# An S5 mixer in rounds on one Trainium2 core: y loaded by GpSimd, weights and rounds regrouped, heads transposed one tile later

## The chip, the core and the metric

The kernel runs on one core of one Trainium2 chip. Its engines are TensorE (PE in the profile, with its weight loads as PEld), VectorE (DVE), ScalarE (ACT), GpSimd (POOL) and SyncE (SP); ACT, POOL and SP also issue DMAs. The metric is the device time of one launch in microseconds (us), the median of several runs.

## The reference

A trunk of two layers on x (1024 tokens by 1024 features, float32). Each sub-layer is a RMS norm with shift, scale and gate from a conditioning vector c. Cut to what matters here:

```python
def _s5_mixer(h, w_in, ..., D, w_glu, b_glu, w_out):
    u, z = jnp.split(h @ w_in, 2, axis=-1)
    ...
    _, _, s_r, s_i = lax.associative_scan(_cplx_combine, (a_r, a_i, bu_r, bu_i), axis=1)
    y = einsum(s_r, C_re) - einsum(s_i, C_im) + D * u      # 64 groups of 16 channels, 64 states each
    y = jax.nn.gelu(y)
    y = y * jax.nn.sigmoid(y @ w_glu + b_glu)
    y = y * jax.nn.silu(z)
    return y @ w_out

x = x + gate * s5(x)
k, v, F = shared_kv(x, c)      # k per head RMS normed
x = x + gate * fox(x, k, v, F) # q = h @ w_in per head RMS normed; attention with forget gates F
```

## The kernel before

Every large product is made of float32 operands split in two: a high part by a copy on ACT (aH, w_hi, wvh) and a low part by a subtraction on DVE (aL, w_lo, wvl), and three matmuls for each block of 128 (high by high, low by high, high by low). The program has these stages in time: a prelude (statistics, the modulation of c, tables of powers); the S5 stage with the projections u and z; the gate projection (pj_g); the output projection (pj_o); values, then keys, then queries (tkps, token tiles); the attention with z of the second layer filled in; the last projection.

**The S5 stage.** The 1024 channels make eight groups, and round e works on group e (`for e in range(KT)`). In a round:
- DVE runs `scan` (L687, over the chunks of 8 tokens, NCH = 128 of them), whose result has its two halves of 64 partitions swapped by two DMAs of SP (`swap_halves`, `DMA v<-v` in the profile). It runs `products` for later groups: wm, and moa, in halves hb = 0 and 1. `rotate_back` (L218, the tensor r) needs the swap. `tables` makes sines of the turning angle: xhi + ylo, then a rounding by adding and taking off a large number (L598) and a subtraction, so that the angle lies in half a turn either way; ACT then takes Abs, Sin, Sin.
- PE runs `turn_in` (transposes of wm, tensor pin, L634), `taps` (pk, L646, reads moa), `states_in` (vps), and `states_out` (py, L706, reads r and moa).
- ACT applies GELU to py, and POOL stores the result to DRAM in eight DMAs (`y_d<-r`, L714).

Between these PE fills in the projections u of groups 1 to 7 and then z of groups 0 to 7, which don't depend on the round. A strip of 128 columns of u or z (L266) has three chunks, of 258, 512 and 256 columns, 24 matmuls each; `unit(n)` puts n chunks at a place of the round. A round has three or four of them. A chunk of u is scaled into `et` by DVE (L374); one of z is copied into `ez` by ACT (L406), two `ez` sharing three buffers with `et`, and each half strip of z is stored by a DMA of SP (`z_d<-ez`). A strip's weights come as `weight_strip` (L87 load, L95 w_hi, L103 w_lo), where the scheduler places them.

**What sets the order.** A tile framework schedules the program: instructions go to their engine's queue in an order that it chooses, and buffers and data give the waits. Two chains written by hand bind it: `ve` puts the DVE steps of the rounds in a row, `te` the PE steps (`order[0]`, `order[1]`). `tc.issue_after(x)` makes what is issued within it stand behind x in the order; it is no wait on a result. Each engine takes its queue in order.

**After the rounds**, the GELU'd y is loaded back (`yl`, eight DMAs of 128x1024 floats, L797), behind the last load of u in the order, split into aH and aL, and multiplied by the gate weights (pj_g, L114).

**Keys and queries** (L941 tkps, L965 hsq, L970 hnt, L977 trps, L981 kh). A token tile is 24 matmuls of 256 columns into PSUM; ACT squares it (hsq), DVE reduces, POOL makes the inverse root, DVE writes the normed tile hnt, which frees the PSUM. When four token tiles are done, `qk_half` transposes them on PE (trps), and ACT and DVE write high and low parts (kh, kl), which are stored. While queries begin, ACT also makes aH of the modulated inputs (L186) and wvh, the high part of the next wide weights (L924), DVE the low part wvl (L925).

Of the kernel before, what the change touches and what calls it, by code (L numbers as in the profile page):

```python
# [20 lines left out]
P = 128  # L21
# [25 lines left out]
def trunk(tc, a, out):  # L47
# [3 lines left out]
    with top:  # L51
# [155 lines left out]
        with l0:  # L207
# [23 lines left out]
            tpi = halves("tpi", 2 * PI_LO, -2 * PI_LO)  # L231
# [135 lines left out]

            def width(c):
                return 512 if c == 0 else 256
# [7 lines left out]
            def u_strip(e, w=None, done=(), ets=(), tags=(None,) * 3):  # L377
                w = w or weight_strip(a["a_w_in"][e], [P, KT, P])
                ut = s5.tile([P, TC, NCH], F32, name="ut", tag="ut")
                bi = s5.tile([P, 1], F32, name="bi", tag="bi", bufs=3)  # L380
                for c in (2, 0, 1):
                    et, m = None, None
                    if c < 2 and ets:
                        et = ets[c]
                    else:
                        ps, m = (done[c], None) if c < 2 and done else chunk(w, c, f"u{e}", tags[c])
# [77 lines left out]

            turn = ta
            S.activation(turn[:, 1:], th[:, 1:], AF.Copy, scale=1.0 / (2 * math.pi))
            turn = [turn[:, i + 1].unsqueeze(2) for i in range(7)]
            ylo = s5.tile([P, NG, 16], F32, name="ylo", tag="ylo")
            xhi = s5.tile([P, NG, 8], F32, name="xhi", tag="xhi")
            S.activation(ylo[:, :, 0:1], turn[0], AF.Copy, scale=-1.0)  # L470
# [115 lines left out]
            def swap_halves(o, x, q=S):  # L586
                for hh in range(2):
                    q.dma_start(out=o[64 * hh:64 * hh + 64], in_=x[64 - 64 * hh:128 - 64 * hh])


            def tables(e, st):
# [6 lines left out]
                V.tensor_scalar(out=cT, in0=sT, scalar1=MAGIC, scalar2=-MAGIC, op0=ALU.add, op1=ALU.add)  # L598
# [77 lines left out]
            def scan(e, st):  # L676
# [12 lines left out]
                swap_halves(r3, r2, Q)  # L689
# [8 lines left out]
            def states_out(e, st, sin):  # L698
# [14 lines left out]
                for i in range(TC):  # L713
                    G.dma_start(out=y_d[e, :, i, :].rearrange("(c g) k -> c g k", c=GC), in_=yb[GC * i:GC * i + GC])  # L714
                st.clear()
                return end

            loaded, sts, order = [], [{} for _ in range(KT + 2)], [None, None]
# [10 lines left out]
            def te(f, *xs):  # L729
                with behind(1):  # L730
                    order[1] = f(*xs)
# [4 lines left out]

            load_u(0, sts[0])
            unit(2)
# [12 lines left out]
            unit()  # L751
            for e in range(KT):
# [3 lines left out]
                unit()  # L756
                if more:
# [3 lines left out]
                    unit(2)  # L761
                    ve(products, e + 1, 1, b_)
                    te(turn_in, 1, b_)
                    te(taps, e + 1, 1, b_)
# [5 lines left out]
                if e % 2 == 0 or not more:  # L770
                    unit(1 if more else 3)
# [21 lines left out]
            for k in range(KT):  # L793
                pool, tag = ((s5, "bb"), (s5, "bbs"), (s5, "x1m"), (s5, "x2m"), (sbm, "min_"), (s5, "ut"), (sb, "uu"), (sb, "uu"))[k]
                yls.append(pool.tile([P, TC, NCH], F32, name=f"yl{k}", tag=tag, bufs=2 if tag == "uu" else 1))
                with tc.issue_after(loaded[-1]):
                    last_y = Q.dma_start(out=yls[k], in_=y_rows(k)).ins  # L797
# [5 lines left out]
            wg = [weight_strip(a["a_w_glu"][e], [P, KT, P], V) for e in range(2)]  # L803
# [102 lines left out]
        with l1a:  # L906
# [9 lines left out]

            wide_dma, last_kl, last_nt, last_sq, last_pow = [], [], [], [], []

            def wide(src, f_src=None):
# [4 lines left out]
                S.activation(wh[:, :, 0:256], raw, AF.Copy)  # L924
                V.tensor_tensor(out=wl[:, :, 0:256], in0=raw, in1=wh[:, :, 0:256].bitcast(F32), op=ALU.subtract)  # L925
# [7 lines left out]
            def token_tile(w, t, nv=256):  # L933
# [4 lines left out]
                for k in range(KT):  # L938
                    hh, ll = act[0][k][i][:, c0:c0 + P], act[1][k][i][:, c0:c0 + P]
                    for at, wt in ((hh, wh), (hh, wl), (ll, wh)):  # L940
                        T.matmul(ps[:, 0:nv], at, wt[:, k, 0:nv], start=(n == 0), stop=(n == 3 * KT - 1))  # L941
                        n += 1
# [17 lines left out]
            def qk_tile(w, t):  # L960
# [8 lines left out]
                nt = hp.tile([P, 4, HD], F32, name="hnt", tag="hnt", bufs=5)  # L969
# [64 lines left out]
            for j, job in enumerate(("v0", "v2", "k0", "k2", "q0", "q2")):  # L1034
# [19 lines left out]
                for i in range(2):  # L1054
# [7 lines left out]
                    for d in range(2):  # L1062
                        nts = []
                        for t in range(4 * i, 4 * i + 4):
# [24 lines left out]
                        if kind != "v":  # L1089
# [6 lines left out]
                            qk_half(nts, gain, 2 * (n0 + d), i, k_d if kind == "k" else q_d)  # L1096
# [281 lines left out]
```

## Time and profile before

| | |
|---|---|
| median of 3 runs | 1177.03 us (1174.55 to 1177.37) |
| the profiled execution | 1175.35 us, span 1173.5 us |
| mean granted TensorE clock | 0.995 |
| busy: PE, DVE, ACT, POOL | 97%, 71%, 52%, 30% |
| S5 rounds, first scan to the gate projection | 107.88 to 293.31 us |
| bytes read and written in DRAM | 138.21 and 46.27 MB |

The span runs from the first to the last instruction; the profiled execution's time has 1.85 us more around it. Engines are listed by busy time, and a group of instructions by its line, engine, operation and tile. Behind a group or an instruction stands the idle time of its engine just before it, with what ended it. In a table of windows each engine's busy us stands with its instructions; the last three columns are the granted clock (1.00 is full), the share of the DMA engines and the GB/s that they moved.

### The profile page before, as it was taken

What the parts mean: (1) busy time and instruction counts of PE and PEld (TensorE: products, weight loads), DVE (VectorE), ACT (ScalarE), POOL (GpSimd) and SP (SyncE); (2) the same over time, 40 slices, a digit from 0 to 9 for tenths busy, and PEclk for the clock granted to TensorE, in tenths of its full rate; (3) what the DMA queues carried; (4) which work ended last, traced back from release to release, by engine and by line L of the source; (5) the groups of instructions that cost most, each with busy time, mean ns of one, the idle gap of its engine ahead of it and who ended that gap; (6) DMA issues with size and microseconds to landing.
All of it is one profiled execution on the core that took longest, in us unless ns stands there. A gap on an engine that the chain in (4) does not pass through costs nothing.

```text
span 1173.5 us, 20611 instructions
## 1 busy us (share of the span) xinstructions
PE 1142.8 (97%) x7506; PEld 1016.8 (87%) x7506; DVE 838.1 (71%) x1723; ACT 605.7 (52%) x1141; POOL 347.1 (30%) x572
## 2 busy tenths in 40 slices
PE   9999999998999999999999999999999999999998
PEld 7688888888888787999999999988988898887886
DVE  6768999885788875935867755348888888898431
ACT  6665777665533432522332533247777777787210
POOL 2300112112000153211343345434455544544100
PEclk9999999999999999999999999999999999999999
DMA  9664577686875783148853339236565554641151
GB/s 354 214 192 133 143 175 171 152 212 182 303 252 198 264 289 121 72 170 281 301 182 132 114 122 273 105 126 132 114 135 129 125 125 111 150 103 63 53 173 72
DMA packets 94661, 197.11 MB, mean 168 GB/s; under 512 B 17728, under 2 KB 42496, under 8 KB 93024
## 3 DMA queue, kind: packets, MB, share of 16 engines
q1 hardware_dynamic: 86768, 174.17, 50.1%
q0 software_dynamic: 6048, 16.85, 4.7%
q10 hardware_dynamic: 1744, 4.77, 1.8%
q8 instruction: 59, 0.97, 0.3%
q14 instruction: 42, 0.34, 0.1%
HBM read 138.21 MB, written 46.27 MB: 157 GB/s over the span
## 4 chain that ended last, share of the span: by engine, by line
PE 70%; DVE 12%; ACT 8%; DMA 5%; issue 3%; POOL 0%; SPq 0%; ACTq 0%; DVEq 0%
PE tkps L941 23%; PE pj_g L114 7%; PE zb L114 6%; PE pj_o L114 6%; PE pj_f L114 4%; PE tp L1185 4%; PE u L266 3%; PE ov L1191 3%; PE f L114 3%; PE ov L1192 2%; PE sp L1152 2%; PE sp L1153 2%; DMA v<-v 2%; ACT pr L1160 2%; DVE r L218 2%
## 5 line engine op out<-in xcount | busy, mean ns | idle before, releaser
L941 PE MATMUL tkps<-wvh,aH 128*128 128x256 f32 (+1 forms) x768 | 220.1, 287 | 3.3 <-DVE hnt L970 3.3
L941 PE MATMUL tkps<-wvl,aH 128*128 128x256 f32 (+1 forms) x768 | 216.6, 282 | 0.0
L941 PE MATMUL tkps<-wvh,aL 128*128 128x256 f32 (+1 forms) x768 | 216.0, 283 | 0.0
L941 PEld LDWEIGHTS tkps<-wvh,aH 128*128 128x128 f32 x768 | 145.2, 189 | 4.1 <-DVE hnt L970 3.7
L941 PEld LDWEIGHTS tkps<-wvl,aH 128*128 128x128 f32 x768 | 145.3, 189 | 0.3 <-issue 0.2
L941 PEld LDWEIGHTS tkps<-wvh,aL 128*128 128x128 f32 x768 | 144.9, 189 | 0.5 <-DVE hmod L183 0.2
L1162 POOL TENSOR_SCALAR pr<-pr,sm 128x128 f32<-128x128 f32 (+7 forms) x128 | 95.2, 750 | 92.7 <-DVE sm L1161 92.6
L1187 ACT ACTIVATE pth<-tp 128x512 fp32r<-128x512 f32 (+1 forms) x192 | 86.8, 489 | 50.5 <-PE ov L1191 29.5
L1160 ACT ACTIVATE pr<-pr,mx 128x128 f32<-128x128 f32 (+7 forms) x128 | 98.9, 774 | 24.9 <-DVE mx L1157 23.9
L1188 DVE TENSOR_TENSOR ptl<-tp,pth 128x512 fp32r<-128x512 f32 (+1 forms) x192 | 101.0, 551 | 9.7 <-ACT pth L1187 8.8
L714 POOL DMA_DIRECT2D y_d<-r x64 | 33.4, 550 | 199.2 <-ACT r L709 198.1
L1157 DVE CUSTOM_DVE_ANT_0 pr<-sp,msk 128x512 f32<-128x512 f32 (+3 forms) x128 | 72.6, 569 | 21.4 <-PE tp L1185 15.5
L1185 PE MATMUL tp<-ident,pr 128*128 128x128 f32 x576 | 82.1, 273 | 2.6 <-DVE ptl L1188 2.6
L1191 PE MATMUL ov<-pth,vhl 128*128 128x256 f32 x320 | 84.1, 296 | 0.3
L965 ACT ACTIVATE hsq<-tkps 128x256 f32<-128x256 f32 x64 | 24.4, 384 | 115.1 <-PE tkps L941 112.5
L95 ACT ACTIVATE w_hi<-w_raw 128x1024 fp32r<-128x1024 f32 x47 | 49.6, 1055 | 64.8 <-PE pj_f L114 19.8
L1192 PE MATMUL ov<-ptl,vhl 128*128 128x256 f32 x320 | 79.7, 283 | 0.2
L1185 PEld LDWEIGHTS tp<-ident,pr 128*128 128x128 f32 x576 | 68.6, 140 | 12.3 <-DVE ptl L1188 2.0
L968 POOL TENSOR_TENSOR hms<-hms,nhalf 128x4 f32<-128x4 f32 x64 | 70.8, 1106 | 5.3
L1152 PE MATMUL sp<-kk,qs 128*128 128x256 f32 (+2 forms) x192 | 69.9, 367 | 0.6 <-DVE mx L1157 0.5
L1153 PE MATMUL sp<-kk,q 66*128 66x256 f32 (+2 forms) x192 | 65.6, 345 | 0.0
L266 PE MATMUL z<-aH,w_hi 128*128 128x258 f32 (+2 forms) x192 | 62.7, 327 | 1.4 <-ACT ez L406 1.4
(356 smaller groups left out, 3154.2 us busy)
## 6 DMA issues: line engine op xcount, KB each, us to landing
modw<-modw SPq DMA_DIRECT2D x48, 512.0 KB
wvr<-kvq_w SPq DMA_DIRECT2D x12, 1024.0 KB
w_raw<-a_w_in SPq DMA_DIRECT2D x16, 512.0 KB
v_d<-vt POOLq DMA_DIRECT2D x32, 256.0 KB, 4.1
kk<-k_d SPq DMA_DIRECT2D x16, 512.0 KB
vhl<-v_d SPq DMA_DIRECT2D x16, 512.0 KB
qs<-q_d SPq DMA_DIRECT2D x32, 256.0 KB
w_raw<-a_w_out SPq DMA_DIRECT2D x10, 512.0 KB
```

Source lines behind the costliest of these rows:

```text
L114: m = T.matmul(ps, w[wt][:, k, :], act[at][k][half], start=(k == k0 and n == 0), stop=(k == k1 and n == 2)).ins
L266: m = T.matmul(ps[:, 0:c1 - c0], w[wt][:, k, :], act[at][k][i][:, c0:c1], start=(k == 0 and n == 0), stop=(k == KT - 1 and n == 2)).ins
L941: T.matmul(ps[:, 0:nv], at, wt[:, k, 0:nv], start=(n == 0), stop=(n == 3 * KT - 1))
L1152: T.matmul(sp[:, 0:wm_], qsl, kk[:, 0, lo:lo + wm_], start=True, stop=False)
L1153: sp_end.append(T.matmul(sp[:, 0:wm_], q1_[:, P * i:P * i + P], kk[0:HD + 2, 1, lo:lo + wm_], start=False, stop=True).ins)
L1160: S.activation(pr[:, 0:nk], pr[:, 0:nk], AF.Exp, scale=-1.0, bias=mx, accum_out=sm)
L1162: G.tensor_scalar(out=pr[:, 0:nk], in0=pr[:, 0:nk], scalar1=sm, scalar2=0.0, op0=ALU.mult, op1=ALU.add)
L1185: T.transpose(out=tp[:, b, :], in_=prs[qi][:, P * (b0 + b):P * (b0 + b) + P], identity=ident)
L1187: S.activation(pth[:, 0:m, dst], tp[:, 0:m, :], AF.Copy)
L1188: V.tensor_tensor(out=ptl[:, 0:m, dst], in0=tp[:, 0:m, :], in1=pth[:, 0:m, dst].bitcast(F32), op=ALU.subtract)
L1191: T.matmul(ov, vhl[:, b, :], pth[:, b - b0, :], start=(b == 0), stop=False)
L1192: end = T.matmul(ov, vhl[:, b, :], ptl[:, b - b0, :], start=False, stop=(b == nb - 1)).ins
```

## The change

It has four parts.
- **Rounds.** A chunk of u or z is now made in two halves of four blocks (`chunk2`, 12 matmuls each), and `unit` counts halves: seven in a round, with one of them between the second `turn_in` and `taps`. A strip's weights are tied into the DVE chain (`load_weights`): the next strip's are loaded, and their parts made, where a strip begins.
- **Wrapped turns.** The angles are kept in 0 to -1 turns, wrapped after each addition by one operation ((s <= -1) + s, L483 after), in place of the rounding by a large number and its subtraction. ACT's three operations get other scales and biases. The small tables xhi and ylo of the prelude are wrapped after each of their five additions.
- **y's loads.** Seven of the eight yl are issued by GpSimd, in the order behind the stores of round 6 (the seventh), the eighth by SP; of the last round's eight stores four go to SP. The gate's first weights stand behind the last round's swap in the order.
- **Keys and queries.** `qk_half` of four token tiles is issued behind the matmuls of the next job's first token tile, and not at once (`turned`); wvh and wvl are made in two halves each; hnt has six buffers for five.

```diff
+            def chunk2(w, c, nm):
+                ps = pj.tile([P, HL], F32, name=f"{nm}_{c}", tag="pj")
+                for r in range(2):
+                    yield ps, in_part(ps, w, c, range(KT // 2 * r, KT // 2 * r + KT // 2))
...
             def z_strip(e):
-                w = weight_strip(a["a_w_in"][8 + e], [P, KT, P], l_eng=V)
+                w = next_weights()
...
-                    ps, m = chunk(w, c, f"z{e}")
+                    two = chunk2(w, c, f"z{e}")
+                    yield next(two)[1]
+                    ps, m = next(two)
...
+            def wrap(o, s):
+                return V.scalar_tensor_tensor(out=o, in0=s, scalar=-1.0, in1=s, op0=ALU.is_le, op1=ALU.add)
...
                 tt(t[:, :, m:2 * m], t[:, :, 0:m], turn[i].broadcast_to([P, NG, m]), ALU.add)
+                wrap(t[:, :, m:2 * m], t[:, :, m:2 * m])
...
-                V.tensor_scalar(out=cT, in0=sT, scalar1=MAGIC, scalar2=-MAGIC, op0=ALU.add, op1=ALU.add)
-                end = tt(sT, sT, cT, ALU.subtract)
-                S.activation(cT, sT, AF.Abs)
-                S.activation(cT, cT, AF.Sin, scale=-2 * PI_LO, bias=hpi)
-                st["sin"] = S.activation(sT, sT, AF.Sin, scale=tpi).ins
+                end = wrap(sT, sT).ins
...
+                S.activation(cT, sT, AF.Abs, bias=half)
+                S.activation(cT, cT, AF.Sin, scale=2 * PI_LO, bias=nhpi)
+                st["sin"] = S.activation(sT, sT, AF.Sin, scale=ntpi, bias=npi).ins
...
-                    G.dma_start(out=y_d[e, :, i, :].rearrange("(c g) k -> c g k", c=GC), in_=yb[GC * i:GC * i + GC])
+                    q = Q if e == KT - 1 and i % 2 else G
+                    stored[e] = q.dma_start(out=y_d[e, :, i, :].rearrange("(c g) k -> c g k", c=GC), in_=yb[GC * i:GC * i + GC]).ins
+                    if q is Q:
+                        stored[KT] = stored[e]
...
+            def load_weights(e):
+                with behind(0):
+                    in_w.append((e, weight_strip(a["a_w_in"][e], [P, KT, P])))
+                order[0] = parts[1].ins
...
+            def next_weights():
+                if not in_w:
+                    load_weights(U_FIRST)
+                e, w = in_w.pop(0)
+                if e + 1 < 2 * KT:
+                    load_weights(e + 1)
+                return w
...
                 ve(scan, e, a_)
-                unit()
+                unit(2)
                 if more:
                     load_u(e + 1, b_)
                     te(turn_in, 0, b_)
                     te(taps, e + 1, 0, b_)
-                    unit(2)
+                    unit(3)
                     ve(products, e + 1, 1, b_)
                     te(turn_in, 1, b_)
+                    unit()
                     te(taps, e + 1, 1, b_)
...
-                if e % 2 == 0 or not more:
-                    unit(1 if more else 3)
+                unit(1 if more else 6)
...
-                with tc.issue_after(loaded[-1]):
-                    last_y = Q.dma_start(out=yls[k], in_=y_rows(k)).ins
+                with tc.issue_after(stored[KT if k == KT - 1 else KT - 2]):
+                    last_y = (Q if k == KT - 1 else G).dma_start(out=yls[k], in_=y_rows(k)).ins
...
-            wg = [weight_strip(a["a_w_glu"][e], [P, KT, P], V) for e in range(2)]
+            with tc.issue_after(swapped[0]):
+                wg = [weight_strip(a["a_w_glu"][e], [P, KT, P], V) for e in range(2)]
...
-                S.activation(wh[:, :, 0:256], raw, AF.Copy)
-                V.tensor_tensor(out=wl[:, :, 0:256], in0=raw, in1=wh[:, :, 0:256].bitcast(F32), op=ALU.subtract)
+                for ks in (slice(0, KT // 2), slice(KT // 2, KT)):
+                    S.activation(wh[:, ks, 0:256], raw[:, ks], AF.Copy)
+                    V.tensor_tensor(out=wl[:, ks, 0:256], in0=raw[:, ks], in1=wh[:, ks, 0:256].bitcast(F32), op=ALU.subtract)
...
+                                if turned and t % 4 == 0:
...
+                                    with tc.issue_after(last_tk[0]), tc.issue_after(last_sq[-1]):
+                                        qk_half(*turned.pop())
...
-                            qk_half(nts, gain, 2 * (n0 + d), i, k_d if kind == "k" else q_d)
+                            turned.append((nts, gain, 2 * (n0 + d), i, k_d if kind == "k" else q_d))
+                            if job == "q2" and i and d:
+                                qk_half(*turned.pop())
```

Three places of the built program show what this does to the engines' queues. The first is DVE at the start of the fifth round, from the scan (L687 before, L712 after) on; wm and moa are the products, rvr, rvi and pwr their tables, w_raw a strip's weights. Before:

```order
L687 SCALAR_TENSOR_TENSOR v_2170<-dT,r_2165 128x1024
L218 TENSOR_TENSOR wm<-bb,rvr 128x64x7
L218 TENSOR_TENSOR tm<-bbs,rvi 128x448
L218 TENSOR_TENSOR moa<-x1m,pwr 128x4x128
L218 TENSOR_TENSOR wm<-wm,tm 128x64x7
L103 TENSOR_TENSOR w_lo<-w_raw,w_hi 128x1024
```

After:

```order
L712 SCALAR_TENSOR_TENSOR v_2187<-dT,r_2182 128x1024
L103 TENSOR_TENSOR w_lo<-w_raw,w_hi 128x1024
L218 TENSOR_TENSOR wm<-bb,rvr 128x64x7
L218 TENSOR_TENSOR tm<-bbs,rvi 128x448
L218 TENSOR_TENSOR moa<-x1m,pwr 128x4x128
L218 TENSOR_TENSOR wm<-wm,tm 128x64x7
```

w_lo moved from behind wm to right behind the scan. It stands there in six of the seven rounds that have products behind the scan; in the fourth it stands behind the products, ahead of `rotate_back`.

The second place is SP and POOL in the last round. z_d<-ez stores half a strip of z, `v<-v x2` is the last swap, `w_raw<-a_w_glu` a gate weight. SP before:

```order
L409 DMA z_d<-ez_2692 128x512
L797 DMA yl_3126<-y_d 128x1024
L797 DMA yl_3128<-y_d 128x1024
L87 DMA w_raw<-a_w_glu 128x1024
L588 DMA v_2872<-v_2871 64x1024 x2
L409 DMA z_d<-ez_2882 128x512
```

SP after:

```order
L426 DMA z_d<-ez_2707 128x512
L612 DMA v_2872<-v_2871 64x1024 x2
L87 DMA w_raw<-a_w_glu 128x1024
L426 DMA z_d<-ez_2896 128x512
L426 DMA z_d<-ez_2897 128x512
L87 DMA w_raw<-a_w_glu 128x1024
L740 DMA y_d<-r_2997 128x1x128 x4
```

POOL after:

```order
L740 DMA y_d<-r_2836 128x1x128 x8
L843 DMA yl_3126<-y_d 128x1024
L843 DMA yl_3128<-y_d 128x1024
L843 DMA yl_3130<-y_d 128x1024
L843 DMA yl_3132<-y_d 128x1024
L843 DMA yl_3134<-y_d 128x1024
L843 DMA yl_3136<-y_d 128x1024
L843 DMA yl_3138<-y_d 128x1024
L740 DMA y_d<-r_2997 128x1x128 x4
```

The two loads of y and the gate weight that stood ahead of the last swap on SP are gone from there (four more loads of y stood further up, two further down); seven loads stand on POOL between the stores of the seventh and of the eighth round.

The third place is ACT where queries begin: hsq squares a token tile, aH is the high part of a modulated input, wvh of weights, kh of transposed heads (lines 965 and 981 are 1014 and 1030 after). Before:

```order
L924 ACTIVATE wvh<-wvr 128x8x256
L981 ACTIVATE kh<-trps,vecs 128x512 x2
L965 ACTIVATE hsq<-tkps 128x256
L186 ACTIVATE aH_1_7054<-x_0_3239,sh_b 128x512
L965 ACTIVATE hsq<-tkps 128x256
```

After:

```order
L973 ACTIVATE wvh<-wvr 128x4x256 x2
L1014 ACTIVATE hsq<-tkps 128x256
L186 ACTIVATE aH_1_7056<-x_0_3247,sh_b 128x512
L1030 ACTIVATE kh<-trps,vecs 128x512 x2
L1014 ACTIVATE hsq<-tkps 128x256
```

One hsq and one aH now stand between wvh and kh, which is still ahead of the next hsq.

More of the change, by code (lines that the diff above doesn't have):

```diff
@@ L230, in trunk @@
             sg_mp = halves("sg_mp", -1.0, 1.0)
-            tpi = halves("tpi", 2 * PI_LO, -2 * PI_LO)
+            ntpi = halves("ntpi", -2 * PI_LO, 2 * PI_LO)
+            npi = halves("npi", -PI_LO, PI_LO)
+            half = halves("half", 0.5, 0.5)
+            nhpi = halves("nhpi", -math.pi / 2, -math.pi / 2)
             hpi = halves("hpi", math.pi / 2, math.pi / 2)
@@ L377, in u_strip @@
             def u_strip(e, w=None, done=(), ets=(), tags=(None,) * 3):
-                w = w or weight_strip(a["a_w_in"][e], [P, KT, P])
+                split_in = w is None
+                w = w or next_weights()
                 ut = s5.tile([P, TC, NCH], F32, name="ut", tag="ut")
@@ L385, in u_strip @@
                     else:
-                        ps, m = (done[c], None) if c < 2 and done else chunk(w, c, f"u{e}", tags[c])
+                        if split_in:
+                            two = chunk2(w, c, f"u{e}")
+                            yield next(two)[1]
+                            ps, m = next(two)
+                        else:
+                            ps, m = (done[c], None) if c < 2 and done else chunk(w, c, f"u{e}", tags[c])
                         if c == 2:
@@ L398, in z_strip @@
             def z_strip(e):
-                w = weight_strip(a["a_w_in"][8 + e], [P, KT, P], l_eng=V)
+                w = next_weights()
                 ez = [s5.tile([P, TC, 64], F32, name=f"ez{i}", tag="et", bufs=3) for i in range(2)]
                 for c in (2, 0, 1):
-                    ps, m = chunk(w, c, f"z{e}")
+                    two = chunk2(w, c, f"z{e}")
+                    yield next(two)[1]
+                    ps, m = next(two)
                     if c == 2:
@@ L462, in trunk @@
             S.activation(cs, tb[:, 0], AF.Sin, scale=-1.0, bias=hpi)
+            def wrap(o, s):
+                return V.scalar_tensor_tensor(out=o, in0=s, scalar=-1.0, in1=s, op0=ALU.is_le, op1=ALU.add)
             turn = ta
             S.activation(turn[:, 1:], th[:, 1:], AF.Copy, scale=1.0 / (2 * math.pi))
+            V.tensor_scalar(out=tb[:, 1:], in0=turn[:, 1:], scalar1=0.0, scalar2=-1.0, op0=ALU.is_gt, op1=ALU.mult)
+            tt(turn[:, 1:], turn[:, 1:], tb[:, 1:], ALU.add)
             turn = [turn[:, i + 1].unsqueeze(2) for i in range(7)]
@@ L469, in trunk @@
             xhi = s5.tile([P, NG, 8], F32, name="xhi", tag="xhi")
-            S.activation(ylo[:, :, 0:1], turn[0], AF.Copy, scale=-1.0)
+            V.tensor_scalar(out=ylo[:, :, 0:1], in0=turn[0], scalar1=-1.0, scalar2=-1.0, op0=ALU.mult, op1=ALU.add)
             G.memset(ylo[:, :, 1:2], 0.0)
@@ L587, in swap_halves @@
                 for hh in range(2):
-                    q.dma_start(out=o[64 * hh:64 * hh + 64], in_=x[64 - 64 * hh:128 - 64 * hh])
+                    last = q.dma_start(out=o[64 * hh:64 * hh + 64], in_=x[64 - 64 * hh:128 - 64 * hh]).ins
+                return last
             def tables(e, st):
@@ L735, in unit @@
                     te(lambda: next(strips, order[1]))
+            in_w = []
+            def load_weights(e):
[9 more added lines that the diff above has]
+                return w
             load_u(0, sts[0])
-            unit(2)
+            unit(4)
             ve(products, 0, 0, sts[0])
@@ L750, in trunk @@
             ve(products, 1, 0, sts[1])
-            unit()
+            unit(2)
             for e in range(KT):
@@ L755, in trunk @@
                 ve(scan, e, a_)
-                unit()
+                unit(2)
                 if more:
@@ L940, in token_tile @@
                     for at, wt in ((hh, wh), (hh, wl), (ll, wh)):
-                        T.matmul(ps[:, 0:nv], at, wt[:, k, 0:nv], start=(n == 0), stop=(n == 3 * KT - 1))
+                        last_tk[:] = [T.matmul(ps[:, 0:nv], at, wt[:, k, 0:nv], start=(n == 0), stop=(n == 3 * KT - 1)).ins]
                         n += 1
@@ L968, in qk_tile @@
                 last_pow.append(G.tensor_tensor(out=ms, in0=ms, in1=nhalf, op=ALU.pow).ins)
-                nt = hp.tile([P, 4, HD], F32, name="hnt", tag="hnt", bufs=5)
+                nt = hp.tile([P, 4, HD], F32, name="hnt", tag="hnt", bufs=6)
                 last_nt.append(V.tensor_tensor(out=nt, in0=pv, in1=ms.unsqueeze(2).broadcast_to([P, 4, HD]), op=ALU.mult).ins)
```

6 lines of the change are left out of this document (4 added, 2 removed).

## The prediction

> **What bounds the kernel now.** I read the page first, then PE's waits, then the S5 rounds in windows, and last the two places where PE's clock falls.
>
> ```profile
> PE 1142.8 (97%) x7506; PEld 1016.8 (87%) x7506; DVE 838.1 (71%) x1723; ACT 605.7 (52%) x1141; POOL 347.1 (30%) x572
> ```
>
> PE is the bound. The change removes no matmul, so it can win only what is left of the span, 1173.5 - 1142.8 = 30.7 us, and what a slow clock costs inside the busy time. PE's waits say who owns the idle time (total, times, longest):
>
> ```profile
> PE py L706 <- DVE r L218: 5.9, 5, 3.4
> PE tkps L941 <- DVE hnt L970: 3.3, 2, 2.7
> ...
> PE u L266 <- DVE et L374: 2.0, 2, 1.1
> PE pk L646 <- DVE moa L218: 1.9, 3, 1.1
> PE z L266 <- ACT ez L406: 1.4, 1, 1.4
> ...
> PE pk L646 <- DVE r L682: 0.9, 2, 0.5
> ...
> PE pk L646 <- ACT moa L620: 0.3, 1, 0.3
> ```
>
> py, pk, z and one u (1.1) belong to the S5 rounds: 5.9 + 1.9 + 0.9 + 0.3 + 1.4 + 1.1 = 11.5 us. The tkps row, 3.3 us, belongs to keys and queries. The change aims at these 14.8 us.
>
> Five rounds, from one scan's start to the next, show why PE waits:
>
> ```profile
> 154.60:176.36 21.76, 21.76 (x161) 19.28 (x159) 20.86 (x26) 15.78 (x26) 4.36 (x9) 1.00 0.71 179
> 176.36:197.93 21.57, 20.24 (x158) 18.11 (x155) 20.88 (x27) 15.03 (x25) 3.85 (x8) 1.00 0.68 159
> 197.93:223.68 25.75, 24.64 (x195) 22.77 (x194) 22.17 (x28) 18.42 (x30) 7.37 (x15) 1.00 0.71 164
> 223.68:246.19 22.51, 20.15 (x151) 17.69 (x151) 21.00 (x28) 15.12 (x24) 3.32 (x7) 1.00 0.61 144
> 246.19:267.54 21.35, 20.66 (x147) 18.43 (x146) 17.35 (x22) 13.22 (x19) 0.83 (x2) 1.00 0.89 237
> sum 112.94, PE 107.46 PEld 96.29 DVE 102.27 ACT 77.57 POOL 19.73; mean PE 21.49 PEld 19.26 DVE 20.45 ACT 15.51 POOL 3.95
> ```
>
> After the length come PE, PEld, DVE and ACT. Rounds with three chunks of projection leave PE with 20.2 us of work against 20.9 on DVE, so PE waits; the round with four has 24.6 on PE, and there DVE waits (its groups in that round; behind the second bar the idle time and what ended it):
>
> ```profile
> L103 DVE TENSOR_TENSOR w_lo<-w_raw,w_hi 128x1024 fp32r<-128x1024 f32 x2 | 2.4, 1220 | 0.9 <-ACT w_hi L95 0.9
> ...
> L218 DVE TENSOR_TENSOR moa<-x1m,pwr 128x512 f32<-128x512 f32 x2 | 1.4, 687 | 2.1 <-PE py L706 2.1
> ...
> L598 DVE TENSOR_SCALAR cT<-sT 128x1024 f32<-128x1024 f32 x1 | 0.7, 693 | 0.0
> ```
>
> Both engines are nearly full and lose to the unevenness: 112.94 - 107.46 = 5.5 us of PE in these rounds.
>
> **The change part by part.** *Rounds with half chunks, tied weight parts, wrapped turns.* From the chain that ended last (start, length, engine or DMA, line):
>
> ```profile
> 131.28 5.68 PE u L266 x24
> ...
> 147.37 2.90 PE z L266 x24
> 157.47 4.74 DMA v<-v
> 179.23 5.55 DMA v<-v
> 249.05 6.72 DMA v<-v
> 270.42 6.61 DMA v<-v
> 293.31 87.21 PE pj_g L114 x375
> ```
>
> A chunk of 512 columns is 5.68 us, one of 256 or 258 is 2.90. By the order of the matmuls, the projection between two py groups is now 11.3, 14.2, 11.3, 16.9, 11.3 and 14.1 us in the six middle rounds, and would be 12.7, 12.7, 12.6, 14.1, 14.1 and 12.7. The wrap puts one operation in place of L598 and a subtraction, so DVE loses 0.69 us a round: 20.9 becomes 20.2, under PE's mean 21.5. That closes py and pk waits. Against it: w_lo (1.22) now stands right behind the scan, ahead of the products whose wm the second transposes (pin) read, and by the order PE reaches that pin 9.4 to 10.8 us after the last py, where it took 12.3 to 13.0. pk has a half chunk (1.4 to 2.8 us) of cover behind pin, pin has none. Each of six rounds may so wait 0 to 1.22 us there; I take the middle, 0.6, hence 3.6. Of z's 1.4 for ez, behind table loads and GELU on ACT, nothing is moved for sure: half stays, 0.7. In the fourth round the store of a half z stands ahead of the scan's swap on SP, and z's first chunk now ends later: between 0 and 2.6 us (the half chunk of 2.8 between), mostly covered; 1.0. Without the last wait (3.45, below) the rounds have 11.5 - 3.45 = 8.05; 5.3 stay. **Gain 2.75** (from -1, if all six wait 1.22 and z keeps 1.4, to 7).
>
> *y's loads by GpSimd.* The last round, from the chain and the timelines (in brackets the wait and what ended it):
>
> ```profile
> 266.35 0.94 SPq L797 DMA_DIRECT2D yl<-y_d  x2
> ...
> 277.12 1.22 DVE L218 TENSOR_TENSOR sT<-sT,v 128x1024 f32<-128x1024 f32 x1 [6.03 <-DMA v<-v]
> ...
> 279.66 0.49 PE L706 MATMUL py<-r,moa 128*128 128x128 f32 x2 [3.45 <-DVE r L218]
> ```
>
> The scan's swap took 6.61 and 6.72 us in the two rounds that hold y's loads, 4.74 and 5.55 in two without: about 1.5 less. With 0.69 from the wrap PE's last wait falls from 3.45 to 1.25. **Gain 2.2** (0.7, swap as slow as now, to 3.45). The loads leave SP; on GpSimd they stand behind the seventh round's stores and ahead of four of the eighth's, whose other four go to SP. What hides them is the last two and a half z chunks, 9.9 us, and after those the first gate projection, which now runs without a break from 293.31. If that cover fails, see the slower rival. The gate weights tied behind the swap are not late: their first user is that same projection.
>
> *The clock.* The granted clock stands behind the busy times in windows of some 2 us:
>
> ```profile
> 279.60:282.00 2.40, 2.34 (x15) 2.34 (x16) 1.21 (x3) 0.61 (x1) 0.00 (x0) 0.72 0.49 147
> 282.00:284.00 2.00, 2.00 (x11) 2.00 (x11) 0.00 (x0) 0.60 (x1) 0.00 (x0) 0.50 0.64 227
> 679.60:682.00 2.40, 2.32 (x12) 2.32 (x13) 2.10 (x5) 0.00 (x0) 1.87 (x3) 0.58 0.07 26
> 682.00:684.50 2.50, 2.50 (x18) 2.50 (x18) 0.76 (x2) 0.15 (x1) 0.00 (x0) 0.72 0.02 7
> 243.00:247.00 4.00, 2.63 (x16) 2.16 (x15) 2.80 (x4) 3.72 (x6) 4.00 (x8) 1.00 0.60 91
> ```
>
> After the wait of 3.45 us PE loses 2.40 x 0.28 + 2.00 x 0.50 = 1.67 us to the clock, after the one of 2.7 us 2.40 x 0.42 + 2.50 x 0.28 = 1.71; in the window with z's wait of 1.4 it loses nothing. A last wait of 1.25 lies below that. **Gain 1.67** (0 if over 2.7 us remain). [...]
>
> *Keys and queries one tile later.* From ACT's and DVE's timelines where queries begin:
>
> ```profile
> 668.54 1.91 ACT L924 ACTIVATE wvh<-wvr 128x2048 fp32r<-128x2048 f32 x1
> 673.87 1.27 ACT L981 ACTIVATE kh<-trps,vecs 128x512 fp32r<-128x512 f32 x2 [3.42 <-PE trps L977]
> 676.70 0.38 ACT L965 ACTIVATE hsq<-tkps 128x256 f32<-128x256 f32 x1 [1.56 <-PE tkps L941]
> ...
> 670.48 2.29 DVE L925 TENSOR_TENSOR wvl<-wvr,wvh 128x2048 fp32r<-128x2048 f32 x1 [0.96 <-ACT wvh L924]
> ```
>
> On ACT kh waits 3.42 us for transposes, and the squares (hsq) of tiles long finished queue behind it; without their squares the norms don't free PSUM, and PE stops at 679.68. Now kh stands one hsq later, and wvl comes in halves of about 1.15, so the norm of the last tile isn't held by 2.29. By the order the transposes come half a tile past the second new tile there, so one hsq still waits: I leave 0.6 of the 3.3 us, and the clock's 1.71 goes. **Gain 4.4** (2.0 to 5.0). The halves add an instruction's start each on ACT and DVE, which are not full here; hnt's sixth buffer covers the tile held longer.
>
> Nothing else is on the path. The prelude's extra turns are some ten small operations on DVE, at most ten times 0.69, at a place where no PE wait is for them; if their cover fails, 1 us.
>
> **Sum.** 2.75 + 2.2 + 1.67 + 4.4 = 11.0 us. The profiled execution took 1175.35 (span 1173.5 and 1.85 around it): 1164.3. The median of the runs, 1177.03, is 1.7 higher: 1166.0.
>
> **The rivals.** *Tied weights hurt.* If w_lo behind the scan is paid in full (1.22 in six rounds, z's wait kept, 1.0 on SP), 9.7 stay and the rounds' gain is 8.05 - 9.7 = -1.65 in place of 2.75: 1170.4. For it: DVE is 96% busy in the windows at 154.60 and 176.36. Against: if PE is behind anyway the wait moves nothing.
>
> *The loads are not behind the last swap.* Nothing makes GpSimd wait for that swap, only for the stores of the round before. If they collide the swap keeps 6.61, the last wait is 3.45 - 0.69 = 2.8, and the slow clock stays: 1.5 + 1.67 less, 1169.2.
>
> *Slower: GpSimd's loads come late.* [...] The page's DMA issues (KB each, us to landing), then POOL's timeline, have:
>
> ```profile
> are<-A_re POOLq DMA_DIRECT2D x2, 16.0 KB, 6.2
> ...
> x_d<-x POOLq DMA_DIRECT2D x16, 256.0 KB, 3.7
> ```
>
> ```profile
> 271.71 1.05 POOL L714 DMA_DIRECT2D y_d<-r  x2 [0.98 <-issue]
> ```
>
> If each of seven loads went only when the one ahead had landed, at 6.2 us, they would end at 272.76 + 43.4 = 316.2, with a split behind (1.3) 317.5; PE needs the seventh 18 matmuls of 512 columns (4.2 us) into the projection, at 297.5. It would wait 20 us and lose 1.7 to the clock: 1166 + 21.7 = 1187.7, slower. It decides from 7t = 297.5 - 1.3 - 272.76 + 11.0 - 1.7, so t = 4.7 us a load. Against it: x_d, half the size, lands in 3.7, and GpSimd issues the next transfer after 0.5 us without waiting. [...]
>
> *No change*: several of these together, the rounds at -1.65, the last wait with its clock as in the second rival, keys and queries at 2.0: 11.0 - 4.4 - 3.2 - 2.4 = 1.0, so 1176.
>
> **How the numbers follow.** Forecast 0.52 (1166); tied weights 0.18 (1170.4); collision 0.12 (1169.2); no change 0.10 (1176); late loads 0.08 (1187.7). The best ends of the terms sum to 7 + 3.45 + 1.67 + 5.0 = 17.1, 1160; the range, 1160 to 1173.5, takes in the first three cases, 0.82. About 0.3%, 3.5 us, is what a measurement of this kernel can tell from no change: faster 0.82, same 0.10, slower 0.08.
>
> **What would show it.** PE's waits for r and moa in the rounds should sum to under 5 us, with rounds of even length; the last swap at about 5 us and a clock of 1.00 behind it; y's seven loads landed before the projection begins; no tkps wait over 1 us. A PE wait for wm at pin in every round would show the tied weights at fault; a long wait of the gate projection for aH or aL would show the loads late, and the forecast wrong.

## The result, and the profile after

| | before | after |
|---|---|---|
| median | 1176.17 us (6 runs, 1174.55 to 1177.64) | 1167.28 us (6 runs, 1164.76 to 1172.73) |
| ratio | | 0.9935, 95% interval 0.9913 to 0.9956 |
| profiled execution, span | 1175.35, 1173.5 | 1168.8, 1167.0 |

The change makes the kernel 0.65% faster, and the median stands 1.3 us above the forecast of 1166.0. Below the sum the picture is another one. PE's waits of the changed kernel, first in the S5 rounds alone, then from the first key or value tile to attention (us in total, times, longest):

```profile
PE pin L659 <- DVE wm L218: 4.2, 2, 3.2
PE pin L659 <- ACT ez L423: 2.9, 2, 1.8
PE py L731 <- DVE r L218: 1.6, 2, 1.3
PE pk L671 <- ACT moa L645: 1.2, 2, 0.6
PE pin L659 <- ACT ut L406: 0.6, 1, 0.6
PE z L269 <- ACT ez L423: 0.4, 1, 0.4
```

```profile
PE tkps L990 <- DVE hnt L1019: 1.4, 2, 1.2
```

The waits of py, pk, z and u, 11.5 us before, are down to 3.2. But pin, which waited for nothing before, now waits 7.7 us, so that the rounds lose 10.9 us in all. The rows put a part of it down to ez and ut on ACT; in the timeline wm ends 0.14 to 0.15 us ahead of each of these transposes as it does ahead of those put down to wm (227.19 against 227.34 in the sixth round, 203.26 against 203.41 in the fifth). All five wait for wm. They stand in rounds two, three, five, six and seven; in the fourth, where w_lo stands behind the products, pin doesn't wait. DVE and then ACT in the fifth round, with the longest of these waits (start, length, then in brackets the idle time and what ended it):

```profile
195.47 2.29 DVE L712 TENSOR_TENSOR_SCAN v<-dT,r 128x1024 f32<-128x1024 f32 x1
199.83 1.22 DVE L103 TENSOR_TENSOR w_lo<-w_raw,w_hi 128x1024 fp32r<-128x1024 f32 x1 [2.07 <-ACT w_hi L95]
200.97 0.62 DVE L218 TENSOR_TENSOR wm<-bb,rvr 128x448 f32<-128x448 f32 x1
...
202.64 0.62 DVE L218 TENSOR_TENSOR wm<-wm,tm 128x448 f32<-128x448 f32 x1
```

```profile
197.79 1.05 ACT L705 ACTIVATE dT<-dec 128x1016 f32<-128x1016 f32 x1 [0.53 <-DVE v L712]
198.75 1.04 ACT L95 ACTIVATE w_hi<-w_raw 128x1024 fp32r<-128x1024 f32 x1
```

DVE stands still for 2.07 us with four products ready behind it in its queue. It waits for w_hi, which on ACT stands behind the copy of dT, which waits for the scan that DVE has just ended. So the tied w_lo can't begin before 2 us after the scan here, and the wm that PE needs comes 3.3 us later than it could: it ends 7.8 us behind the scan's start, and 4.5 in the untied kernel below, where no w_lo stands ahead of it in this round. The chain that ended last now runs through these steps (start, length):

```profile
198.75 1.05 ACT w_hi L95
199.83 1.22 DVE w_lo L103
222.60 1.07 ACT w_hi L95
223.69 1.23 DVE w_lo L103
```

The granted clock, behind this wait, behind the last wait of the rounds, and where queries begin (third number from the end):

```profile
203.40:206.00 2.60, 2.59 (x14) 2.60 (x15) 2.57 (x4) 0.81 (x2) 0.00 (x0) 0.59 0.52 180
206.00:208.00 2.00, 2.00 (x19) 1.39 (x18) 2.00 (x3) 0.92 (x2) 0.00 (x0) 0.68 0.00 0
...
277.80:280.00 2.20, 2.16 (x19) 2.16 (x20) 1.12 (x1) 0.31 (x2) 0.00 (x0) 1.00 1.03 417
...
675.40:678.00 2.60, 2.55 (x22) 2.58 (x23) 1.52 (x4) 0.47 (x1) 1.39 (x3) 1.00 0.73 278
```

The two slow stretches that the prediction showed are gone, and a new one stands behind the wait at pin: 2.60 x 0.41 + 2.00 x 0.32 = 1.7 us. (Each profile has one more in the prelude, also of 1.7 us, at 16 to 22 us before and at 56 to 62 us after.)

By stage, from the starts of the first matmuls: the gate projection begins at 291.2 (before 293.1), values, keys and queries take 472.8 to 770.1, 297.3 us (before 475.7 to 776.4, 300.7). Of the span's 6.5 us 2.0 were won up to the gate projection, 0.9 between there and the values, 3.4 in values, keys and queries and 0.2 behind them.

### The profile page after: what moved, and what is told of

The parts are those of the page before. It is cut to its first block, busy times and chain, and to the rows that moved or that the text cites. A ratio compares the mean times of both kernels' runs of the same rounds, so it can differ in the third digit from the quotient of the medians.

```text
span 1167.0 us, 20630 instructions
## 1 busy us (share of the span) xinstructions
PE 1139.6 (98%) x7506; PEld 1015.0 (87%) x7506; DVE 838.2 (72%) x1735; ACT 609.1 (52%) x1152; POOL 350.1 (30%) x581
## 4 chain that ended last, share of the span: by engine, by line
PE 78%; DVE 9%; ACT 6%; DMA 5%; issue 2%; POOL 0%; SPq 0%; ACTq 0%; DVEq 0%
PE tkps L990 23%; PE pj_g L114 8%; PE pj_o L114 8%; PE zb L114 6%; PE u L269 5%; PE pj_f L114 4%; PE tp L1240 4%; PE z L269 3%; PE ov L1246 3%; PE f L114 3%; PE ov L1247 3%; DMA v<-v 2%; PE sp L1207 2%; PE sp L1208 2%; ACT pr L1215 1%
## 5 line engine op out<-in xcount | busy, mean ns | idle before, releaser
L1019 DVE TENSOR_TENSOR hnt<-tkps,hms 128x256 f32<-128x256 f32 x64 | 27.0, 422 | 53.7 <-POOL hms L1017 53.6
```

## The experiments

The ratios are to the kernel before, with the interval behind. Edits are against the changed kernel unless the text says otherwise; lines left out of them are marked by three dots.

### The tie, and how soon PE comes to pin

**Untied weights.**

```diff
             def load_weights(e):
-                with behind(0):
-                    in_w.append((e, weight_strip(a["a_w_in"][e], [P, KT, P])))
-                order[0] = parts[1].ins
+                in_w.append((e, weight_strip(a["a_w_in"][e], [P, KT, P])))
```

> The changed kernel with the strips' weights no longer tied into VectorE's chain; all else as changed. Theory (the tied low part holds the transposes): in the changed kernel PE's waits at pin sum to 7.7 us and all end when wm does, which stands behind w_lo on DVE. Untied, w_lo stands ahead of the rounds' wm in the first, second and sixth round only, so pin's waits fall to 0 to 2.5 us, and without the wait of 3.24 us the slow clock behind it (1.7 us) goes too: about 1160 to 1162 in place of 1167.3. Rival (PE simply comes to pin sooner, since half a chunk moved from ahead of pin to behind it): pin's waits stay over 6 us and the time stays at 1166 to 1168.

Measured: 1162.79 us, 0.9890 (0.9867 to 0.9912), span 1160.7. PE's waits in its rounds:

```profile
PE pin L659 <- DVE biz L421: 1.3, 1, 1.3
PE py L731 <- DVE r L218: 1.2, 1, 1.2
PE pin L659 <- ACT ez L423: 1.2, 1, 1.2
PE pin L659 <- ACT ut L406: 0.6, 1, 0.6
...
PE pin L659 <- DVE wm L218: 0.2, 1, 0.2
```

pin's waits fell from 7.7 to 3.3 us, less far than expected, and the slow clock in the fifth round went. The two longest of those left, 1.3 and 1.2 us, again end when wm does, in the two rounds in which the scheduler itself put w_lo ahead of wm. The gate projection begins 6.5 us sooner (284.7). The tie costs this kernel about 0.45%.

**Tied, but behind the products.** Load and high part stay where a strip begins; the subtraction is put into the chain between the products and `rotate_back`, or where its own strip begins if that comes first.

```diff
...
+            def low_part():
+                while due:
+                    raw, hi, lo = due.pop(0)
+                    with behind(0):
+                        order[0] = V.tensor_tensor(out=lo, in0=raw, in1=hi.bitcast(F32), op=ALU.subtract).ins
...
                     te(states_in, e + 1, b_)
+                low_part()
                 ve(rotate_back, a_)
...
```

> The changed kernel with the weights still tied, but their low part put behind the products of the second half and ahead of rotate_back, where DVE waits for the swap anyway; load and high part are made where a strip begins, as changed. Theory (the tied low part holds the transposes): pin's waits fall from 7.7 us to under 1.5 (the first round still has a w_lo ahead), no py wait is added since the swap is waited for there, the slow clock of the fifth round goes: about 1159 to 1161. Rival (PE comes to pin sooner): pin's waits stay over 6 us, 1166 to 1168.

Measured: 1169.66 us, 0.9948 (0.9928 to 0.9968): no gain, so the expected time was wrong. pin's waits did go, and others came, for r and for the low part itself (PE's waits in the rounds, then DVE in the fourth round):

```profile
PE py L731 <- DVE r L218: 4.5, 2, 3.6
PE u L269 <- DVE w_lo L784: 3.1, 1, 3.1
PE z L269 <- DVE w_lo L784: 1.6, 1, 1.6
...
PE pin L659 <- DVE wm L218: 0.6, 3, 0.2
```

```profile
183.87 1.22 DVE L784 TENSOR_TENSOR w_lo<-w_raw,w_hi 128x1024 fp32r<-128x1024 f32 x1
189.86 1.23 DVE L784 TENSOR_TENSOR w_lo<-w_raw,w_hi 128x1024 fp32r<-128x1024 f32 x1 [4.78 <-ACT w_hi L95]
191.00 1.22 DVE L218 TENSOR_TENSOR r<-cT,v 128x1024 f32<-128x1024 f32 x1
```

In the fourth round a strip begins just ahead of this place, so that the high part of the one after it isn't made yet: its load is issued at 185.11, and on ACT it stands behind a copy that waits 3.22 us for PE. DVE waits 4.78 us for it before it may go on to `rotate_back`, and PE then 3.60 us for r. So the wait at pin does come from what stands ahead of wm, as the theory has it. But the cause is wider than w_lo's place against the products: at this fixed place too DVE waits for a load and for ACT, and something that PE needs stands behind it.

**The rounds as before** (whole chunks, their order, untied weights; wrap, y's loads, keys and queries as changed):

```diff
...
-                w = next_weights()
+                w = weight_strip(a["a_w_in"][8 + e], [P, KT, P], l_eng=V)
...
-                    two = chunk2(w, c, f"z{e}")
-                    yield next(two)[1]
-                    ps, m = next(two)
+                    ps, m = chunk(w, c, f"z{e}")
...
-                unit(1 if more else 6)
+                if e % 2 == 0 or not more:
+                    unit(1 if more else 3)
...
```

> The changed kernel with the order of the rounds, whole chunks and untied weights as before, but with the wrapped turns, y's loads by GpSimd and the keys and queries as changed. Theory (the tied low part makes the new rounds a net loss): pin waits go, the py and pk waits of before come back less 0.69 us for each by the wrap, 4 to 6 us in all against 9.5 plus 1.7 of slow clock: 1160 to 1163, faster than the changed kernel. The prediction's own first term (half chunks and tied weights gain 2.75 with the wrap): slower than the changed kernel, 1168 to 1171.

Measured: 1162.67 us, 0.9894 (0.9873 to 0.9916). The prediction's first term expected a loss; without the new rounds the kernel is faster. **The rounds as before, with the weights tied**, the same but for `next_weights()` in the strips:

> The changed kernel with whole chunks in the order of the rounds as before, but with the strips' weights tied into VectorE's chain as changed (the wrap, y's loads, keys and queries as changed). Untied it ran at 1162.7. Theory (the tie costs by itself, since DVE stands still for the high part and then does 1.2 us of w_lo ahead of products or rotate_back): 1165.5 to 1168, with waits for wm, moa or r of 2 to 5 us more than untied. Rival (the tie only hurts where half a chunk less stands ahead of pin): 1162 to 1164.

Measured: 1168.75 us, 0.9944 (0.9926 to 0.9962). PE's waits in its rounds:

```profile
PE pin L652 <- ACT ez L416: 3.9, 2, 2.1
PE pk L664 <- DVE moa L218: 2.0, 3, 0.7
PE vps L689 <- ACT min__1439 L653: 1.8, 1, 1.8
```

The row puts the two waits at pin (2.13 and 1.76 us) down to ez, but here too wm ends 0.15 us ahead of each. They stand in the fourth and the fifth round, in which w_lo, ahead of wm on DVE, waits longest for w_hi:

```profile
181.26 1.23 DVE L103 TENSOR_TENSOR w_lo<-w_raw,w_hi 128x1024 fp32r<-128x1024 f32 x1 [2.60 <-ACT w_hi L95]
206.16 1.23 DVE L103 TENSOR_TENSOR w_lo<-w_raw,w_hi 128x1024 fp32r<-128x1024 f32 x1 [3.37 <-ACT w_hi L95]
```

DVE waits for w_hi in the untied kernels as well. Up to the last r of the rounds these waits sum to 2.3 us before, 0.7 with half chunks untied and 2.9 tied, 1.9 with whole chunks untied and 6.0 tied. So what such a wait costs hangs on what stands behind it in the queue.

With the changed kernel these make a square: half chunks 0.9935 tied and 0.9890 untied, whole chunks 0.9944 tied and 0.9894 untied. The tie costs 0.45 to 0.5% with either (neither pair of intervals overlaps), and the half chunks make no difference that these runs can tell.

**Pin later.** The half chunk between the second transposes and the taps is put ahead of the transposes, with tied weights, then with untied ones:

```diff
                     ve(products, e + 1, 1, b_)
+                    unit()
                     te(turn_in, 1, b_)
-                    unit()
```

> The changed kernel with the half chunk that stands between the second transposes (pin) and the taps (pk) put ahead of the transposes; weights tied as changed. Theory (the tied low part): the products are as late as now, so the wait moves from pin to pk, which needs moa 1.4 us after wm: where the half chunk is 1.4 us long nothing is won, where it is 2.8 us 1.4 is: pin and pk together 5 to 6 us, about 1165. Rival (PE comes to pin sooner, and that is all): pin and pk together fall under 3.5 us, and the time to 1160 to 1162.

> The changed kernel with the weights untied and the half chunk between pin and pk put ahead of pin: both edits that won alone. Theory (two causes, the tie that holds DVE and the missing cover ahead of pin): the untied kernel has 3.5 us of pin waits left in its rounds, the half chunk ahead takes the two of 1.3 and 1.2 us away and gives pk 0.5 to 1 us more: about 1160.5 to 1162 against 1162.8 and 1162.9 alone. Rival (both edits cure the same waits): no better than either alone, 1162.5 to 1164.

Measured: tied 1162.92 us, 0.9894 (0.9871 to 0.9916); untied 1163.28, 0.9884 (0.9860 to 0.9908). Tied, the waits in the rounds are:

```profile
PE z L269 <- ACT ez L423: 2.1, 2, 1.4
PE pk L671 <- DVE moa L218: 2.0, 3, 0.7
PE pin L659 <- ACT ez L423: 1.8, 1, 1.8
PE pk L671 <- ACT moa L645: 1.0, 1, 1.0
PE py L731 <- DVE r L218: 1.0, 1, 1.0
```

pin and pk together wait 4.9 us, near what the theory gave, while the time came out nearer to the rival's. Both edits together are no better than either: with half chunks they cure the same loss, as the second rival had it.

All waits in the tied kernel's rounds sum to 8.0 us, 2.9 less than in the changed kernel, the slow clock behind pin is still there, and yet the span is 4.5 us shorter. In these two profiles the slow stretch of the prelude makes up the rest: the changed kernel's has it, this one's hasn't. The medians are 4.4 us apart too, though, so some 1.5 us between them stay open.

With whole chunks, where pin stands as late in the round, the tie still cost 0.5%. The traces show what is common: the wait left at pin here (1.8 us, in the fifth round) and the two with whole chunks all stand behind a w_lo that waited 2 us or more for w_hi (2.06, 2.60, 3.37). So a later pin seems to cover w_lo's own 1.2 us, and not that wait. That the tie costs is shown; this split of its cost is read from the traces, and no run separates the two.

### The other parts

**The wrap alone**, on the kernel before:

```diff
-                V.tensor_scalar(out=cT, in0=sT, scalar1=MAGIC, scalar2=-MAGIC, op0=ALU.add, op1=ALU.add)
-                end = tt(sT, sT, cT, ALU.subtract)
+                end = wrap(sT, sT).ins
...
```

> The kernel before with the wrapped turns alone: one operation of DVE for two in each round's tables, 0.69 us less, and some ten small operations more in the prelude. The prediction's step (DVE and PE are both near full in the rounds, so the 0.69 closes py and pk waits): waits in the rounds fall from 11.5 by 2.5 to 5 us, the last from 3.45 to 2.8 with its slow clock kept: 1171.5 to 1174 against 1176.2. Rival (the rounds are set by the order, the wrap is taken up by slack on DVE): 1175 to 1177.

Measured: 1172.51 us, 0.9973 (0.9962 to 0.9984), inside what the prediction's step gave. The waits in the rounds fell from 11.5 to 9.3 us, a little less than expected; the last one stayed at 3.4.

**y's loads alone**, on the kernel before, and **y's loads back on SP**, in the changed kernel, where the edit runs the other way:

```diff
-                with tc.issue_after(loaded[-1]):
-                    last_y = Q.dma_start(out=yls[k], in_=y_rows(k)).ins
+                with tc.issue_after(stored[KT if k == KT - 1 else KT - 2]):
+                    last_y = (Q if k == KT - 1 else G).dma_start(out=yls[k], in_=y_rows(k)).ins
...
```

> The kernel before with y's loads alone changed: seven by GpSimd behind the seventh round's stores, four of the last round's stores on SP, the gate's first weights behind the last swap. The prediction's step (the swap loses 1.5 us, the wait of 3.45 falls to about 2 and its slow clock goes): 1172.5 to 1174. Rival, after the kernel with the loads back on SP was no slower (the swap is as long whoever issues the loads): the swap within 0.6 us of 6.61, the last wait 2.8 to 3.5 us with a slow clock behind it, 1175 to 1177.

> The changed kernel with y's eight loads on SP behind the last load of u, all of the last round's stores on POOL, and the gate's first weights not tied behind the swap, as before; all else as changed. The prediction's step (the loads lengthen the last swap by 1.5 us): the swap goes from 6.06 to 6.6 or more, PE's last wait from 1.35 to about 2.85, and the slow clock behind it (1.67) returns: about 1170.4. Rival (the last wait fell because the scan begins about 1.5 us earlier against PE, through the wrap and w_lo's place, and the swap was hardly shortened): the swap is within 0.6 us of 6.06, the last wait stays between 1.2 and 2.0 us, no slow clock: 1167 to 1168.

Measured: alone 1171.27 us, 0.9969 (0.9958 to 0.9980); taken back 1168.1, 0.9927 (0.9904 to 0.9949), no slower than the changed kernel. The last swap, in the chain of the changed kernel, of y's loads alone, and of the kernel with them back on SP:

```profile
269.15 6.06 DMA v<-v
```

```profile
267.45 5.61 DMA v<-v
```

```profile
271.38 4.15 DMA v<-v
```

Alone, the step holds, though not by the swap alone: the swap went from 6.61 to 5.61, 1.0 us of the 1.5 forecast, the last wait from 3.45 to 1.93, and the clock stays at 1.00 behind it. Taken back in the changed kernel it costs nothing, and the swap took neither of the two lengths expected: 4.15 us, with a last wait of 0.6. SP's timeline with the loads back on it shows why the swap is short there:

```profile
265.73 0.53 SPq L843 DMA_DIRECT2D yl<-y_d  x1
267.15 0.33 SPq L426 DMA_DIRECT2D z_d<-ez  x1
270.82 1.15 SPq L612 DMA_DIRECT2D v<-v  x2
272.06 0.92 SPq L87 DMA_DIRECT2D w_raw<-a_w_glu  x1
```

Before, two loads of y and the gate's weights were issued in the 3.5 us ahead of the swap. Here one load of y stands five us ahead, and the scheduler itself put the weights behind the swap. Another load of y is issued at 255.40, and the swap that ACT issues behind it, ahead of the scan, takes longer than in the changed kernel (5.53 us there):

```profile
259.14 6.78 DMA v<-v
```

The scan then starts 9.7 us behind the start of the py group ahead of it, where it is 8.5 in the changed kernel; that the load does this isn't shown. So this experiment didn't bring the collision with the last swap back, and doesn't say what it would cost.

**Heads at once** (with the halves kept), **whole wvh and wvl** (with the later transposes kept):

```diff
-                            turned.append((nts, gain, 2 * (n0 + d), i, k_d if kind == "k" else q_d))
+                            qk_half(nts, gain, 2 * (n0 + d), i, k_d if kind == "k" else q_d)
...
-                for ks in (slice(0, KT // 2), slice(KT // 2, KT)):
-                    S.activation(wh[:, ks, 0:256], raw[:, ks], AF.Copy)
+                S.activation(wh[:, :, 0:256], raw, AF.Copy)
...
```

> The changed kernel with the four token tiles transposed at once and five hnt buffers, as before, and wvh and wvl still in halves. The prediction's step (kh, waiting for its transposes, holds the squares queued behind it): the tkps wait of 2.7 us with its slow clock of 1.7 us returns, about 1170 to 1171.5. Rival (the halves of wvl were what mattered, the norm was held by 2.29 us of wvl on DVE): the wait stays under 1.5 us, 1167 to 1168.5.

> The changed kernel with wvh and wvl each made by one instruction of 2048 columns, as before, and the heads transposed one tile later as changed. The prediction's step (the place of kh is what mattered): tkps waits stay at 1.4 us or grow by up to 1.1, no slow clock, 1167 to 1168.5. Rival (the halves mattered): the tkps wait grows to over 2.5 us and the slow clock returns, 1170 to 1171.

Measured: 1169.98 us, 0.9941 (0.9924 to 0.9959), and 1169.25, 0.9935 (0.9913 to 0.9957): neither differs from the changed kernel beyond its interval, and both profiles lose 2.8 to 2.9 us to the slow clock behind pin, where the changed kernel's loses 1.7. So the stage itself tells more, from the first tkps to the first matmul of attention: 300.7 us before, 299.0 with halves alone, 298.2 with later transposes alone, 297.3 with both. Either edit alone removes the wait of 2.67 and the slow clock (the longest tkps wait is 1.3 us with the heads at once, 0.7 with wvh and wvl whole). The prediction took kh's place and the halves of wvl as one step; each by itself wins half of the 3.4 us or more.

**Heads two token tiles later**, untied, with seven hnt buffers:

```diff
-                                if turned and t % 4 == 0:
+                                if turned and t % 4 == 1:
...
```

> The changed kernel with untied weights (1162.8 alone) and the heads transposed behind the second token tile of the next job, not the first, with seven hnt buffers. Theory (one square still queues behind a kh that waits for its transposes): the tkps waits of 1.24 and 0.18 us go, 1160.5 to 1162. Rival (the norm waits for wvl on DVE, not for the square behind kh): the waits stay, 1162 to 1164.

Measured: 1162.4 us, 0.9892 (0.9875 to 0.9909), span 1159.4. PE's waits from values to attention:

```profile
PE tkps L988 <- DVE hnt L1017: 0.7, 2, 0.5
```

The waits halve (1.4 to 0.7) but don't go, which suggests that a part of them was behind kh; one trace doesn't show it. In time it can't be told from the other untied kernels. The kernels with untied weights or a later pin, 1162.4 to 1163.3, all beat both the kernel before and the changed one, by some 1.1% and 0.45% (the intervals of two of them, at 1162.67 and 1162.92, overlap that of the changed kernel by 0.0003).

## Why the prediction was right, and where it was not

The total was right: faster, by a little less than forecast. That it came out so near is in part luck, since the first of its terms was wrong in sign. By its terms (profiled executions; forecast, then measured):

- **Rounds without the last wait and its clock: 2.75 gained; 3.2 lost.** This is the step that failed. "Each of six rounds may so wait 0 to 1.22 us there; I take the middle, 0.6, hence 3.6": pin waits 7.7 us, 3.24 of them in one round. Two things were missed. The bound took w_lo's own 1.22 us as the most it could hold wm up; in its place of the chain it also waits for w_hi, 2.07 us in the fifth round. The prediction's own row of w_lo had such a wait in it, 0.9 us. And a wait that long can slow the clock, 1.7 us here, as its rows of before showed. The lower bound of -1 leaves out the 1.0 us for SP that the rival counts. Of that 1.0 the fourth round shows a py wait of 0.2, and z's wait is 0.4 where 0.7 was left. What was said of DVE's 0.69 us a round held: py, pk, z and u without the last wait fell from 8.1 to 1.8 us, and the wrap alone wins 0.27%. The rival "tied weights hurt", at 1.65 lost, had the place right, if not the wait for w_hi: without the clock the rounds lost 1.5. I gave it 0.18.
- **y's loads: 2.2 gained; 2.1.** PE's last wait is 1.35, where 1.25 was forecast. The way there was partly another: the swap lost 0.55 us and not 1.5. The rest is the scan, which starts 8.5 us behind the start of the py group ahead of it, where it was 10.1 before. Most of that comes with the loads too: with y's loads alone changed it is 8.9, since the swap of the round ahead took 5.60 us and not 6.72, and DVE waited 1.50 us for it and not 2.61. The rival of a collision is half true: the loads leave POOL from 270.35 on, while the swap runs. That they would come late was wrong, and no load waits for the landing of the one ahead, as the rival's sum supposed: POOL issues six within 3.3 us, they land 8.6 to 14.5 us later, side by side and not one behind the other, and the gate projection waits for none:

```profile
270.35 3.33 POOL L843 DMA_DIRECT2D yl<-y_d  x6 [0.29 <-issue]
275.82 0.54 POOL L843 DMA_DIRECT2D yl<-y_d  x1 [2.14 <-DMA y_d<-r]
```

- **The clock: 1.67 gained; 1.67 there**, and lost again in the fifth round, as above.
- **Keys and queries: 4.4 gained; 3.4.** tkps waits 1.4 us in place of the 0.6 that I left.
- **Not in the sum:** 0.9 us in the gate and output projections, where a wait of 0.47 for w_lo went. And 1.4 us up to the gate projection, 1.2 of them PE's busy time there (274.5 against 275.7). No edit can be named as its cause: less the slow stretches that time is 272.3 us before, 271.1 after, 271.1 with y's loads alone and 272.8 untied with pin later, so it differs by more among kernels that have the new rounds or not. It stays open.

The sum of the terms was 11.0, the span gave 6.5. The first term missed by 6.0 us and keys and queries by 1.0; 2.5 us that no term had made up for a part. The medians are 8.9 apart, so the rest of the agreement with 1166.0 is the profiled executions' own place among the runs (1168.8 after lies above its median, 1175.35 below). A reader should take the total as right, partly by luck, and the first term as wrong in sign.

Of the signs that the prediction named, the waits for r and moa came (2.8 us, under 5), as did the clock of 1.00 behind the last swap and y's loads in time. Rounds of even length did not (21.5 to 25.4 us from scan to scan, about as before), nor the swap of 5 us (6.06), nor tkps waits under 1 us (1.2). The sign set for the tied weights, a wait for wm at pin, came in five of seven rounds.

## What to carry to other kernels

Tying a step into an engine's chain ties all that stands behind it to everything the step waits for: price it by its wait for its inputs, not by its own duration, and ask what stands behind it. In the fifth round w_lo waited 2.07 us for w_hi and took 1.22 itself, and PE waited 3.24 us for the wm behind it. When work is moved from ahead of a wait to behind it, the wait ahead loses its cover even if nothing else changes: with tied weights pin waits 7.7 us with the half chunk behind it, and 1.8 with it ahead. Gains measured one at a time need not add: the wrap and y's loads each won 0.3% alone, and with both in place taking the second back cost nothing, though the scheduler then placed the loads otherwise than before.

## What the runs showed of the hardware

How long PE must idle before its clock falls is not one number here. Behind a wait of 1.83 us the clock fell in the kernel with the rounds as before, and behind one of 3.60 us it did not in the kernel with w_lo behind the products:

```profile
275.00:277.00 2.00, 1.86 (x11) 1.86 (x12) 0.08 (x1) 0.00 (x0) 0.54 (x1) 0.72 0.99 367
```

```profile
191.00:194.60 3.60, 0.07 (x1) 0.00 (x0) 3.60 (x5) 0.62 (x1) 0.00 (x0) 1.00 0.77 169
194.60:197.00 2.40, 2.33 (x20) 2.33 (x21) 2.33 (x3) 0.00 (x0) 0.00 (x0) 1.00 0.30 57
```

Waits of 1.93 and 2.18 us went without a fall in two more kernels (y's loads alone, untied with pin later), and one of 2.13 with 0.73 soon behind it led to one (whole chunks, tied). So in these kernels idling of about the same length falls out both ways; what decides between the two, no run here shows.

Nor is the length of the slow stretch one number. Behind the same wait of 3.24 us at pin the clock is low for some 3.4 us in the changed kernel, which costs 1.7 us, and for some 6.8 us in three others, which costs 2.8 to 2.9. With wvh and wvl whole, where the changed kernel is back at 1.00 from 208 us on:

```profile
203.00:206.00 3.00, 2.25 (x11) 2.28 (x12) 2.93 (x5) 0.81 (x2) 0.00 (x0) 0.50 0.68 206
206.00:209.00 3.00, 3.00 (x20) 2.39 (x20) 2.84 (x5) 1.04 (x3) 0.00 (x0) 0.50 0.02 5
```

The longest of these runs' stretches, with whole chunks tied, cost 3.2 us. From these losses I estimate that a wait of 2 to 3.6 us in this kernel is best priced with a chance of 1.7 to 3.2 us more.
